# Casts of weights behind exponentials, modulation columns in another bank, and a different scratch tile, in a two-layer transformer block on one core

## The chip, the core and the metric

The kernel runs on one core of a Trainium2 chip. The core has five engines that run side by side, each through its own instruction queue in order: TensorE (PE; matrix products and transposes, results in PSUM), VectorE (DVE), ScalarE (ACT), GpSimd (POOL), and SyncE (SP), which here only issues DMA transfers. Instructions on different engines are ordered by semaphores. The metric is the device time of one execution in microseconds (us), the median of three runs.

## What is computed

The reference is a block of two layers over 512 latent tokens and 256 context tokens with 1024 features, in float32. Cut to what matters here:

```
for l in range(2):
    mx = silu(c) @ mod_w[l] + mod_b[l]          # 6 x 1024 modulation values, for latents
    mc = silu(c_ctx) @ mod_w[l] + mod_b[l]      # the same for the context
    shx1, scx1, gx1, shx2, scx2, gx2 = split(mx, 6)
    hx = rms(x) * norm_mix_w * (1 + scx1) + shx1
    hc = ...                                    # the context, with mc
    layer 0: heads q, k, v = (hx|hc) @ ev_w_in, rms and rotation of q and k,
             half the heads attend in a window of 128 with a sink, half densely;
             joined heads @ ev_w_out
    layer 1: differential attention: (softmax(q0 k0) - lam * softmax(q1 k1)) @ v
    x = x + gx1 * attention
    x = x + gx2 * swiglu(rms(x) * ... , ffn_w_in, ffn_w_out)
    the context likewise, in layer 0 only
return x
```

The modulation gives, per layer, six parts of 1024 values for each of the two streams: shift, scale and gate for the attention (parts 0, 1, 2) and for the feed-forward part (3, 4, 5). They are independent of the tokens, so they are computed piece by piece beside other work.

## The kernel before, in words

**Precision.** A float32 operand is split into a rounded part (hi) and the rest (lo): ACT casts (`nc.scalar.copy(hi, raw)`), then DVE or POOL subtracts (`tensor_sub(lo, raw, hi)`). A product of two such operands is three products on PE: hi*hi, hi*lo, lo*hi. So each weight tile costs one DMA, one cast on ACT and one subtraction, before PE may use it.

**Who sets the order.** Most of the program is ordered by a planner: it simulates the engines and hands out, on each engine, the ready instruction that stands earliest in the program. Its times are its own, so an instruction can be placed ahead of others in a queue and then, on the chip, hold them while it waits. `tc.manual_schedule(engines={PE})` keeps PE in the order of the program text; it is entered at the sixth tile of layer 0's attention (`i == 5`) and holds to the end. `with behind("exp"):` adds, for the instructions of the block that run on ACT, an edge to the last exponential issued so far: in ACT's queue they come after it. Instructions of other engines and DMAs in that block get no edge.

**Layer 0's attention** runs from about 78 to 396 us. It has four blocks b = 0 to 3 of four query heads with one key and value head (b < 2: window, b > 1: dense), and each block goes over six tiles of 128 tokens in the order 4, 5 (context), 0, 1, 2, 3; the last block in the order 0 to 5. The text speaks of blocks 0 to 3 and of a block's first to sixth tile; `j` counts the tiles from 0. In each step:

- `scores0(i)`, four times, one head each: PE writes the scores `sc` to one of two banks (L587, with mask products L589), DVE takes the row maximum (`mx`, `nm`), ACT the exponential (L601, tile `Pt`). After two heads, DVE takes `rc`, the reciprocal of the sums, and POOL scales `Pt` (L613).
- `transposes0(i - 1)`, three times: PE transposes `Pt` of the tile before (`ppt`, L621, in one of two banks tr0 and tr1), and ACT (L626) and DVE (L624) copy it back.
- `values0(i - 1)`: PE multiplies by the values into `av` (L632, bank acc1), ACT copies to `o` (L634).
- `projected(n)`: quarters of the next block's input projection `inps` (L474, bank acc0), each over two of the eight slices of 128 features. A finished tile is copied (`qkv`), rotated by DVE and POOL, split (`qd`, `kd`), and transposed by PE later (`qpt`, `kpt`, also in tr0 and tr1; copied by ACT as `qt`, `kT`).

In the last block there is no next projection; from its fourth tile on, the output projection `ops` of earlier tiles stands there instead, whose result DVE multiplies by a gate row `g` (`rtmp`, L480).

**Input weights.** `weights0` makes the weights of one block in four units of 256 features: cast on ACT (`wihi`, L507), subtraction on POOL (first and third unit) or DVE (second and fourth) (`wilo`, L508). The loads go into raw tiles (tag "raw", two of them). The first two units of block b + 2 are taken at the end of the fifth tile (`j == 4`) of block b, the other two at the start of the next block (`j == 0`); between them, at the end of the sixth tile, a modulation piece uses the same two raw tiles.

**Output weights.** `out_units0` issues eight loads at its first call, then gives one unit per call: cast (`woh`, L801), subtraction on POOL for the first six and on DVE for the last two (`wol`, L802). In block 3 one unit is taken at the end of the first tile, two in the second, three in the third, the rest in the fourth.

**Modulation pieces.** `mod_steps` makes 256 columns in two steps. First: two DMAs (`modw`, L177) into raw tiles, eight row products (x16 in the trace) to a PSUM tile `mod` in the bank given by `bank` (L182), and ACT's copy `modr` (L185). Then: two small products `modcol` (L191, x4 in the trace), in the same bank, and DVE adds the bias (`modc`, L279). `mod_run(n)` does the first step at the end of a tile (`RUNS`), and `mod_ends()` the second, behind the first scores of the next tile. At the end of block 1 and of block 3's first tile `mod_ends()` follows `mod_run` at once.

**The gate.** `gate_mem(0, 2, 2)` transposes gate columns on PE (`gps`, L293), copies them on DVE (`grow`) and writes them to DRAM (`gmem`, SP); `oproj.gates` loads them back to all partitions (`g`, L306), in the first tile of block 3.

**Layer 1's start.** The first head's projection is laid out by hand, with the normalisation of latent tiles 1, 2, 3 between (`last_norm0`). `factors` squares these three tiles first: ACT's squares (L331) write their elements to one tile, `spare`, that nobody reads; only the row sums count. Then for each tile POOL multiplies by the row factor into `h` (L345, shown as `nh`), PE transposes `h` (`npt`, L352), and DVE and ACT apply scale and shift into `hc` (L360, L358). `h` and `hc` are `spare`, tiles of the ring "xo" (six), or a raw tile.

## Time and profile before

| | us |
|---|---|
| median of 3 runs | 1686.9 (1685.64 to 1687.21) |
| the profiled execution | 1686.72 |
| its span (first to last instruction) | 1684.9 |
| PE busy | 1629.0 (97%) |
| DVE busy | 1145.2 (68%) |
| ACT busy | 934.8 (55%) |
| POOL busy | 713.2 (42%) |

The clock that PE was granted is 0.994 on the mean. Rows of a timeline read: start, duration, engine, line of the kernel, operation, output<-inputs, shape, count, and in a bracket the engine's idle time before it with what released it. Rows of waits read: engine, tile and line that waited, whom it waited for, the total in us, how often, and the longest. An ending q (SPq) means the engine's instruction queue. Idle time is put down to the release that came last. PE's products are pipelined, so their durations overlap.

### The profile page before, as it was taken

The page shows a single profiled execution, that of the slowest core. Times are in us where ns is not written, and L with a number is a line of the kernel's source. Part 1 is how long each engine was busy: PE and PEld are TensorE (multiplying, and loading weights), DVE is VectorE, ACT ScalarE, POOL GpSimd, SP SyncE. Part 2 cuts the span into 40 slices and gives each one's busy share as a digit, 9 for nine tenths or more (in the row PEclk, how much of TensorE's full clock was granted, in tenths as well). Part 3 has the DMA queues.
Part 4 walks back from the last instruction along what each step waited for, and adds up shares of the span by engine and source line. Part 5 has one row for each costly group of instructions (what it writes and reads, how often), then busy time and mean ns, then how long its engine had stood idle before and what let it go on. Part 6 is the DMA issues. An engine that isn't in the chain of part 4 may idle for free. (4 is left out here: it accounts for less than half of the span.)

```text
span 1684.9 us, 28521 instructions
## 1 busy us (share of the span) xinstructions
PE 1629.0 (97%) x10376; PEld 1467.9 (87%) x10376; DVE 1145.2 (68%) x1980; ACT 934.8 (55%) x2008; POOL 713.2 (42%) x872
## 2 busy tenths in 40 slices
PE   6999999899999999999999999999999999999998
PEld 3977787677999999998878799999988899999887
DVE  3765756554799987767767666666666598887433
ACT  5466665745455655544564456666666555555320
POOL 2665555621345554412413367766765332221000
PEclk8999999999999999999999999999999999999999
DMA  9221321421455555439965221111113333331431
GB/s 321 70 71 52 93 70 51 163 63 38 120 178 173 166 159 164 135 110 334 305 185 192 91 58 44 48 42 47 45 51 100 113 96 110 104 105 53 138 100 63
DMA packets 221692, 194.67 MB, mean 116 GB/s; under 512 B 20016, under 2 KB 206960, under 8 KB 221552
## 3 DMA queue, kind: packets, MB, share of 16 engines
q1 hardware_dynamic: 221200, 192.65, 36.9%
q8 instruction: 81, 1.33, 0.3%
q14 instruction: 59, 0.48, 0.1%
q10 hardware_dynamic: 352, 0.21, 0.0%
HBM read 179.94 MB, written 12.87 MB: 114 GB/s over the span
## 5 line engine op out<-in xcount | busy, mean ns | idle before, releaser
L928 ACT CAST wbh<-wr 128x512 fp32r<-128x512 f32 x170 | 104.8, 621 | 122.9 <-PE p L960 67.7
L960 PE MATMUL p<-hT,wbh 128*128 128x256 f32 (+1 forms) x752 | 154.1, 298 | 0.0
L474 PE MATMUL inps<-wih,hT 128*128 128x384 f32 x512 | 143.9, 343 | 2.4 <-ACT qkv L688 1.7
L938 POOL TENSOR_TENSOR wbl<-wr,wbh 128x512 fp32r<-128x512 f32 x43 | 58.9, 1369 | 174.2 <-ACT wbh L928 174.2
L960 PEld LDWEIGHTS p<-hT,wbh 128*128 128x128 f32 x752 | 122.1, 191 | 0.2
L938 DVE TENSOR_TENSOR wbl<-wr,wbh 128x512 fp32r<-128x512 f32 x127 | 107.8, 860 | 19.8 <-ACT wbh L928 15.8
L960 PE MATMUL p<-hT,wbl 128*128 128x256 f32 (+1 forms) x376 | 111.8, 297 | 0.0
L960 PE MATMUL p<-t,wbh 128*128 128x384 f32 (+1 forms) x480 | 110.9, 317 | 0.0
L231 POOL TENSOR_TENSOR modp<-modp 128x512 f32<-128x512 f32 x40 | 57.5, 1437 | 111.8 <-ACT modp L230 111.8
L613 POOL TENSOR_SCALAR Pt<-Pt,rc 128x256 f32<-128x256 f32 (+3 forms) x96 | 75.3, 796 | 66.1 <-DVE rc L610 58.5
L960 PE MATMUL p<-hTt,wbh 128*128 128x256 f32 (+1 forms) x480 | 100.9, 302 | 0.0
L914 POOL TENSOR_TENSOR wr<-wr 128x512 f32<-128x512 f32 x40 | 62.2, 1556 | 91.1 <-DVE ws L919 88.8
L474 PEld LDWEIGHTS inps<-wih,hT 128*128 128x128 f32 x512 | 93.4, 188 | 5.4 <-ACT qkv L688 2.8
L960 PE MATMUL p<-b,wbh 128*128 128x384 f32 x368 | 93.5, 335 | 0.6 <-DVE c L988 0.6
L928 ACT CAST wbh<-ws 128x512 fp32r<-128x512 f32 x120 | 69.5, 580 | 43.7 <-PE p L960 28.5
L224 DVE SCALAR_TENSOR_TENSOR ma<-modw,cols,ma 128x256 f32<-128x256 f32 x140 | 91.5, 654 | 2.3
L601 ACT ACTIVATE Pt<-sc,nm 128x256 f32<-128x256 f32 (+3 forms) x96 | 67.7, 708 | 34.0 <-DVE nm L597 16.0
L474 PE MATMUL inps<-wil,hT 128*128 128x384 f32 x256 | 85.8, 335 | 0.0
L938 DVE TENSOR_TENSOR wbl<-ws,wbh 128x512 fp32r<-128x512 f32 x120 | 81.7, 681 | 1.7 <-ACT wbh L928 1.6
L960 PEld LDWEIGHTS p<-t,wbh 128*128 128x128 f32 x480 | 82.8, 189 | 0.0
L960 PEld LDWEIGHTS p<-hTt,wbh 128*128 128x128 f32 x480 | 78.4, 191 | 3.0 <-ACT modp L230 2.1
L474 PE MATMUL inps<-wihi,hT 128*128 128x384 f32 x256 | 76.6, 356 | 2.1 <-DVE modc L279 1.9
(357 smaller groups left out, 5219.1 us busy)
## 6 DMA issues: line engine op xcount, KB each, us to landing
modw<-in_mod_w_dram SPq DMA_DIRECT2D x96, 512.0 KB, 4.8
wr<-in_ffn_w_in_dram SPq DMA_DIRECT2D x176, 256.0 KB, 3.0
wdr<-in_ffn_w_out_dram SPq DMA_DIRECT2D x66, 512.0 KB, 3.6
wir<-in_od_w_in_dram SPq DMA_DIRECT2D x96, 128.0 KB, 2.3
hidm<-hid SPq DMA_DIRECT2D x44, 192.0 KB, 1.9
hr<-hidm SPq DMA_DIRECT2D x22, 192.0 KB, 3.5
x<-in_x_dram SPq DMA_DIRECT2D x8, 512.0 KB, 3.6
wir<-in_ev_w_in_dram SPq DMA_DIRECT2D x16, 256.0 KB, 3.4
```

The lines of the kernel that those rows point to most:

```text
L224: nc.vector.scalar_tensor_tensor(acc, w[:, k], scale[k], acc, ALU.mult, ALU.add)
L231: nc.gpsimd.tensor_add(pr[:, 0:2], pr[:, 0:2], pr[:, 2:4])
L474: nc.tensor.matmul(ps, hs[j][:, k, :], ws[k // 2][z][:, k % 2, c0:c1], start=(k, j, z) == (0, 0, 0), stop=(k, j, z) == (KT - 1, 1, 0))
L601: turn["exp"] = nc.scalar.activation(p[:, :n], s, AF.Exp, bias=nm[:, c1], accum_out=sm[:, c1])
L613: nc.gpsimd.tensor_scalar(p[:, :n], p[:, :n], rc[:, hh:hh + 1], 1.0, ALU.mult, ALU.mult)
L914: nc.gpsimd.tensor_sub(w, raw[f, "G1"], w)
L928: nc.scalar.copy(hi, w)
L938: (nc.gpsimd if name == "G2" else nc.vector).tensor_sub(lo, raw[need[n]], f32(hi))
L960: nc.tensor.matmul(ps, w[:, k, :], H[b][h][:, k, :], start=first and k == 0 and q == 0, stop=final and k == 3 and q == 2, skip_group_check ...
```

## The change

- `mod_steps` takes a bank for the columns (`cols_bank`); `mod_run` gives acc1, so `mod` stays in acc0 and `modcol` is in acc1.
- At the end of block 1 there is no `mod_ends` and no `gate_mem` any more; the columns are made behind the first scores of block 2, the gate's transpose and write at the end of block 3's first tile. The columns of that tile's piece are made behind the first scores of its second tile.
- `weights0`: the third and fourth unit are taken behind the exponentials of the first and second scores of a block's first tile (the first block takes what it has at the start, as before); the first two units in the fifth tile are behind that tile's last exponential.
- `out_units0`: in block 3's second tile the two units move from behind the first and third to behind the second and fourth exponential; in the third tile they stay behind the first three.
- `last_norm0`, tile 1: `h` is a tile of the ring and `hc` is `spare`; it was the other way round.

```diff
-    def mod_steps(l, part, n, new_tile, pool, bank, wide=None, room=("modr", 1)):
+    def mod_steps(l, part, n, new_tile, pool, bank, wide=None, room=("modr", 1), cols_bank=None):
...
-        pc2 = p_1.tile([P, nb, 2], F32, name="modcol", tag=bank)
+        pc2 = p_1.tile([P, nb, 2], F32, name="modcol", tag=cols_bank or bank)
...
-                mod_runs.append(mod_steps(*mods.pop(0), raw_tile, at.pool, "acc0"))
+                mod_runs.append(mod_steps(*mods.pop(0), raw_tile, at.pool, "acc0", cols_bank="acc1"))
...
             if j == 0 and b < 3:
-                ws += units
+                if not b:
+                    ws += units
...
                 scores0(i)
+                if j == 0:
+                    with behind("exp"):
+                        ws += islice(units, 1)
                 mod_ends()
                 transposes0(i - 1)
                 scores0(i)
+                if j == 0:
+                    with behind("exp"):
+                        ws += units
                 projected(n[0])
...
                 if j == 4 and b < 2:
-                    ws = [next(units) for _ in range(2)]
+                    with behind("exp"):
+                        ws = [next(units) for _ in range(2)]
...
                 mod_run(RUNS[b][j])
-                if b == 1 and j == NT - 1:
-                    mod_ends()
-                    gate_mem(0, 2, 2)
...
                 mod_run(1)
-                mod_ends()
                 wp.close()
...
                 ws = [next(units)]
+                gate_mem(0, 2, 2)
                 oproj = OutProj(0, ws, o_t, xs)
...
             scores0(i)
+            mod_ends()
             if t < 3:
+                with behind("exp"):
+                    ws += islice(units, t - 1)
+                transposes0(i - 1)
+                scores0(i)
                 with behind("exp"):
                     ws += islice(units, 1)
                 transposes0(i - 1)
                 scores0(i)
                 with behind("exp"):
                     ws += islice(units, t - 1)
-                transposes0(i - 1)
                 scores0(i)
                 with behind("exp"):
-                    ws += islice(units, 1)
-                scores0(i)
+                    ws += islice(units, 2 - t)
...
     def last_norm0(t):
-        h, hc = (spare if t == 1 and not i else raw_tile([P, KT, P], "nhc") if t == 2 and i else
+        h, hc = (spare if t == 1 and i else raw_tile([P, KT, P], "nhc") if t == 2 and i else
                  keep.tile([P, KT, P], F32, name="nh", tag="xo", bufs=6) for i in range(2))
```

## The prediction, made before the changed kernel ran

> **What bounds the kernel now.** I read the page first, then the busy time by stretches, then what TensorE (PE) waited for between 78 and 396 us, where layer 0's attention runs, and then the timelines of single engines around each wait. "us" is the time from the span's start.
>
> ```profile
> span 1684.9 us, 28521 instructions
> ...
> 80.00:400.00 320.00, 301.86 (x2146) 241.81 (x2144) 190.35 (x436) 190.93 (x469) 164.87 (x234) 1.00 0.25 78
> ...
> 950.00:1290.00 340.00, 328.87 (x2263) 312.30 (x2261) 224.93 (x443) 223.13 (x568) 230.72 (x359) 0.99 0.19 55
> ```
>
> The columns after the stretch's length are PE, weight loads, VectorE (DVE), ScalarE (ACT), GpSimd (POOL), clock, DMA share and GB/s. PE is busy 301.86 of 320 us, at clock 1.00; no other engine passes 60%, and DMA is at 0.25. So PE sets the end, and only its 18.1 idle us can be won in this stage. Which waits make them up:
>
> ```profile
> PE ppt L621 <- ACT qt L546: 4.6, 5, 2.2
> PE ppt L621 <- POOL Pt L613: 2.9, 5, 1.0
> PE sc L587 <- ACT Pt L601: 2.3, 3, 1.3
> PE inps L474 <- DVE modc L279: 1.9, 3, 1.0
> ...
> PE modcol L191 <- ACT modr L185: 1.0, 2, 0.5
> ...
> 96.92 0.44 PE L474 MATMUL inps<-wihi,hT 128*128 128x384 f32 x1 [1.01 <-DVE modc L279]
> ...
> 110.35 0.45 PE L474 MATMUL inps<-wihi,hT 128*128 128x384 f32 x1 [0.65 <-DVE modc L279]
> ...
> 199.18 0.66 PE L621 MATMUL ppt<-cst,Pt 128*128 128x128 f32 x4 [2.20 <-ACT qt L546]
> ...
> 219.97 0.61 PE L191 MATMUL modcol<-cst,modr 128*128 128x2 f32 x4 [0.49 <-ACT modr L185]
> ...
> 225.41 1.10 PE L621 MATMUL ppt<-cst,Pt 128*128 128x128 f32 x8 [0.89 <-ACT qt L546]
> ...
> 303.97 0.96 PE L587 MATMUL sc<-kT,qt 128*128 128x256 f32 x4 [0.49 <-ACT Pt L601]
> ...
> 310.10 0.61 PE L191 MATMUL modcol<-cst,modr 128*128 128x2 f32 x4 [0.55 <-ACT modr L185]
> ...
> 315.97 0.97 PE L587 MATMUL sc<-kT,qt 128*128 128x256 f32 x4 [1.29 <-ACT Pt L601]
> ...
> 322.00 0.33 PE L621 MATMUL ppt<-cst,Pt 128*128 128x128 f32 x1 [0.34 <-POOL Pt L613]
> ...
> 322.88 0.77 PE L621 MATMUL ppt<-cst,Pt 128*128 128x128 f32 x5 [0.55 <-POOL Pt L613]
> ```
>
> In a bracket stands PE's idle time before the row and what released it. From the attention's sixth tile on, PE's order is the program's own, so each such wait moves the rest of the stage unless something else is late behind it. Before that tile the planner orders PE too.
>
> **Part 1, the columns' bank.** The two small products that make the modulation columns, modcol, write acc0 before, so the next projection, also in acc0, waits for DVE to read them: 1.9 us in three waits. After, they write acc1, whose next writer is av at the tile's end, microseconds later; the projection then needs only the copy modr, which modcol itself had to wait for. No instruction is added. I take **-1.9**. Bounds: 0, if another wait stands right behind, and -1.9.
>
> **Part 2, casts of layer 0's input weights.** The first two casts of the set loaded during block 1 are planned into its fifth tile, in front of an exponential:
>
> ```profile
> 194.90 0.83 ACT L507 CAST wihi<-wir 128x768 fp32r<-128x768 f32 x1 [0.63 <-DMA wir<-in_ev_w_in_dram]
> ...
> 197.03 0.83 ACT L507 CAST wihi<-wir 128x768 fp32r<-128x768 f32 x1 [0.79 <-issue]
> 197.77 0.79 ACT L601 ACTIVATE Pt<-sc,nm 128x640 f32<-128x640 f32 x1
> ...
> 198.55 0.57 ACT L546 CAST qt<-qpt 128x512 fp32r<-128x512 f32 x1
> ...
> 195.81 1.82 POOL L508 TENSOR_TENSOR wilo<-wir,wihi 128x768 fp32r<-128x768 f32 x1 [1.76 <-ACT wihi L507]
> ...
> 196.07 1.84 DVE L535 TENSOR_TENSOR qd<-qy,qd 128x256 fp32r<-128x256 f32 x1 [1.01 <-ACT qd L534]
> ...
> 210.14 0.43 DVE L535 TENSOR_TENSOR qd<-qy,qd 128x256 fp32r<-128x256 f32 x1 [0.27 <-ACT qd L534]
> ...
> 203.52 0.81 ACT L601 ACTIVATE Pt<-sc,nm 128x640 f32<-128x640 f32 x1
> ...
> 218.41 1.07 PE L182 MATMUL mod<-modw,s_pad 128*32 128x256 f32 x16
> ...
> modw<-in_mod_w_dram SPq DMA_DIRECT2D x4, 512.0 KB, 3.5
> ```
>
> ACT stands 0.63 us for the load and 0.79 us before the second cast; with 2 x 0.83 us of casts that is 3.08 us in front of exp and qt, and the copy qt (end 199.12) holds the bank that the transposes at 199.18 want. With the edge both casts come after this tile's last exponential, the one at 203.52, some 7 us later. Without them qt would be through about 2 us or more sooner, and PE reaches the transposes at 196.98. I take **-2.0** of the 2.20. What the late casts hold: their weights aren't read before the next block, but the raw tiles they free are wanted by the next modulation load (modw on SP's queue, 3.5 us to land, products at 218.4); casts from 204.3 on and a subtraction of 1.82 leave until 218.41 some 12 us, of which the load takes 3.5, so the sixth tile's work covers it. If that cover were gone PE would wait in the mod products.
>
> In block 0 the same two casts were planned into the fourth tile:
>
> ```profile
> 110.61 0.84 ACT L507 CAST wihi<-wir 128x768 fp32r<-128x768 f32 x1 [1.69 <-DMA wir<-in_ev_w_in_dram]
> ```
>
> ACT loses 1.69 us there, but PE has projections to do meanwhile; I take **-0.3**, bounds 0 and -1.7.
>
> The third and fourth cast, in a block's first tile, already follow exponentials in the trace, and they hang on a load that can't start before the modulation products have released its raw tile:
>
> ```profile
> 223.58 0.83 ACT L507 CAST wihi<-wir 128x768 fp32r<-128x768 f32 x1 [0.93 <-DMA wir<-in_ev_w_in_dram]
> 224.49 1.82 POOL L508 TENSOR_TENSOR wilo<-wir,wihi 128x768 fp32r<-128x768 f32 x1 [2.20 <-ACT wihi L507]
> ...
> 226.99 0.35 PE L474 MATMUL inps<-wilo,hTc 128*128 128x384 f32 x1
> ```
>
> **Part 3, the columns a tile later.** At the end of block 1 the change takes modcol and the gate's transpose out of the spot at 219.97, where PE idled 0.49 us for modr; behind the next tile's scores modr is long done. Then 0.89 us at 225.41, which sits behind the cast at 223.58, could go too. But here something is late next: the products end at 219.48, the load ends 4.1 us after them, cast and POOL subtraction end at 226.31, and PE reads wilo at 226.99. Whatever PE gains in this tile, it can't read before 226.31: of the 1.38 us at most **0.68** is left, and nothing if cast and qt keep their order. I take **-0.3** for both waits.
>
> At the start of block 3 the same move saves the 0.55 us at 310.10. There the changed casts of the output weights help as well:
>
> ```profile
> 313.50 1.04 ACT L801 CAST woh<-wor 128x1024 fp32r<-128x1024 f32 x1
> ...
> 318.71 2.36 POOL L802 TENSOR_TENSOR wol<-wor,woh 128x1024 fp32r<-128x1024 f32 x1
> ...
> 310.04 3.00 SPq L306 DMA_DIRECT2D g<-gmem  x2
> ...
> 339.71 0.69 DVE L480 TENSOR_TENSOR rtmp<-ops,g 128x512 f32<-128x512 f32 x1 [0.81 <-PE ops L836]
> ```
>
> In the second tile the cast at 313.50 stands ahead of the second exponential, and scores wait 1.29 us for that. The tile before, without such a cast, waits 0.49 at 303.97; so 0.80 goes. Later the subtraction at 318.71 keeps POOL from scaling Pt, 0.34 + 0.55 us at 322; with the casts behind the second and fourth exponential the scaling comes first, or so I read it. Together 0.55 + 0.80 + 0.89 = 2.24; modcol (two products) now lies inside the tile and the gate's transpose is issued here, so I take **-1.9**, bounds -0.5 and -2.2. The gate's round trip through DRAM is now behind the eight weight loads on SP's queue: a write of 8 KB, and the two g loads, issued at 310.04 before, wait for it to land. Behind them stand only the x loads. First use is the rtmp at 339.71, nearly 30 us later, so projections and scores cover it; nothing is charged. If g were later than that, PE would stall at the second output sum.
>
> **Part 4, layer 1.**
>
> ```profile
> 948.88 0.55 POOL L160 TENSOR_TENSOR rs_n<-rs_n,neghalf 128x1 f32<-128x1 f32 x1
> ...
> 953.21 1.06 ACT L331 ACTIVATE nh<-x 128x1024 f32<-128x1024 f32 x1 [1.91 <-DVE x L481]
> ...
> 954.47 1.12 POOL L345 TENSOR_SCALAR nh<-x,rs_n 128x1024 f32<-128x1024 f32 x1 [2.25 <-ACT nh L331]
> ...
> 955.64 1.09 PE L352 MATMUL npt<-cst,nh 128*128 128x128 f32 x8 [1.34 <-POOL nh L345]
> ```
>
> The squares of tiles 1 to 3 all write `spare` as waste, and the scaled rows of tile 1 are written there too; so POOL's scaling at 954.47 waits for tile 3's square (953.21 + 1.06), though tile 1's own factor was done at 949.43. After, the scaled rows have a tile of their own and `spare` takes what is written after the transposes. The scaling can then run before 952, and PE's 1.34 us goes. What comes next is the following weight product, whose operands are there. **-1.3**, bounds 0 (if the other tile of the ring weren't free) and -1.34.
>
> **A price for what is new.** A moved cast is still 0.83 us (1.04 for the output weights) of ACT and 1.82 or 2.36 of POOL somewhere else. No row shows it at its new place. Bounds: nothing, if it fills idle time (ACT is free 40% of the stage), and 2.20 a place, as in block 1's fifth tile. Five places change: block 0's and block 1's fifth tile, the first tiles of blocks 1 and 2, block 3's second. I take **+1.5**, two waits a little under the 0.89 of 225.41: that row is the nearest, a cast behind an exponential, as all are after the change.
>
> Here a rule speaks against the change. The row: DVE's subtraction qd took 1.84 us beside POOL's wilo and ended with it, against 0.43 alone. The Trainium skill, page "SBUF — State Buffer", section "Who interferes with whom", says that a DVE instruction with two SBUF inputs and a GpSimd instruction that reads SBUF exclude each other for a whole instruction; the trace agrees with 1.84 against 0.43. By it each of the five moved subtractions could cost DVE 1.4 us; if PE paid all of that, 7.0 would stand in place of the 1.5 and the sum would be -0.7.
>
> **Sum.** -1.9 - 2.0 - 0.3 - 0.3 - 1.9 - 1.3 + 1.5 = -6.2 us. The profiled execution took 1686.72 us (1684.9 of span and 1.8 around it), the median of the runs is 1686.9: 1680.5 on the one, **1680.7** on the other. Gains hold to the end, since PE runs at 97% in 950 to 1290 us and only a load late by microseconds could eat them.
>
> **Rivals.**
> - **Floors and the planner eat the layer-0 gains.** ACT, DVE and POOL are ordered by the planner anew; the edge only forbids a cast ahead of an exponential, which in the first tiles already holds, so there the change does nothing. If the waits at 199 and 316 turn into others of the same size, the bank (1.9) and layer 1 (1.3) stay, less 1.5: -1.7, **1685.2**. For it: the floor at 226.31, and POOL's part in the waits. Against: the 2.20 us has two plain culprits that leave. Chance 0.27.
> - **Slower: moved casts and subtractions stall PE where they land.** Place: the end of each fifth tile and the sixth tile behind it, and the like in blocks 2 and 3. A 1.82 us subtraction on POOL holds DVE's two-input additions of the projection as qd was held (1.4 us), the row maximum queued behind them on DVE comes late, the exponential and the score bank after it, and PE waits as at 199.18. Price 2.20 in five places is 11.0, against gains of 7.7: +3.3, **1690.2**. It decides from 1.54 us a place. Against: a tile's third scores stand behind eight transposes and half a projection, which gives the first exponential slack. Chance 0.11.
> - **More goes than the named waits.** Of the 4.6, 2.9 and 2.3 us in the list of waits the rows name 3.09, 0.89 and 1.78; 4.0 us are other waits for the same qt, Pt and exp. If 3 of them go with the rest, and no new wait comes, it is 10.7: **1676.2**. Chance 0.10.
>
> **How the numbers follow.** Forecast (-9 to -3.4 us) 0.52. About 0.2%, 3.4 us, is what a measurement of this kernel can tell from no change. Faster by more: 0.52 + 0.10 = 0.62; within it 0.27; slower 0.11. The range leaves out half of the larger gain and most of the slower case: 1676.5 to 1688.5.
>
> **What would show it.** In the changed profile: no wait of modcol's bank or modr before inps and modcol (part 1, 3); no wait above 0.5 us for qt in block 1's fifth tile, and its two casts behind the fourth exponential (part 2); inps still reading wilo about 7 us after the mod products (the floor); the wait for the exponential near 314 at 0.5 us; the transposes of layer 1's tile 1 without a wait for nh (part 4). Wrong if PE waits for weight casts in the sixth tiles, for modw, or for g, or if PE's planned order before the sixth tile comes out longer.

## The result, and the profile after

The changed kernel is slower: 1687.62 us (median of 21 runs, 1683.95 to 1693.22), the kernel before beside it 1684.61 us (21 runs, 1681.51 to 1688.07), ratio **1.002**, interval 1.0012 to 1.0027. A second series of the same two kernels gave 1687.97 and 1685.33 us, 1.0009 (1.0000 to 1.0018). Forecast was -6.2 us; measured are +1.5 to +3.4.

The page's first line of the changed kernel, and the stretches that were shown of before (same columns: length, busy us and count of PE, weight loads, DVE, ACT, POOL, then clock, DMA share, GB/s):

```profile
span 1685.0 us, 28524 instructions
```

```profile
80.00:400.00 320.00, 301.32 (x2122) 239.07 (x2121) 190.21 (x427) 188.69 (x465) 161.62 (x230) 0.99 0.24 76
950.00:1290.00 340.00, 328.89 (x2268) 312.97 (x2266) 225.14 (x444) 223.00 (x568) 230.55 (x360) 0.99 0.19 56
```

The two profiled spans agree to 0.1 us, though the medians differ by 3 us. The reason lies ahead of the first changed place: the change has nothing to do in the first 78 us, but in the changed kernel's profiled execution the clock was better there. The first 78 us of before, then of the changed kernel:

```profile
0.00:78.00 78.00, 62.09 (x394) 50.03 (x394) 41.57 (x83) 39.94 (x80) 29.03 (x46) 0.89 0.67 212
```

```profile
0.00:78.00 78.00, 61.48 (x410) 49.08 (x411) 44.27 (x91) 42.17 (x86) 31.75 (x50) 0.93 0.67 212
```

At 0.93 instead of 0.89 it came to the attention's first scores 2.89 us sooner (75.81 against 78.70). That is no gain of the change: in the profile of x3 below, whose code up to layer 1 is that of before, the first scores start at 75.77. So I count both from there, as in all comparisons of profiles below. Starts of PE's rows in the two traces; the last column is the difference less -2.89:

```
                                     before    after    counted from first scores
first scores of layer 0               78.70    75.81     0
mod products, end of block 0         144.65   142.31    +0.55
mod products, block 1's fourth tile  190.00   187.41    +0.30
mod products, end of block 1         218.41   218.17    +2.65
mod products, block 3's first tile   308.48   308.29    +2.70
first output products                333.15   334.03    +3.78
layer 1's first projection           951.18   952.17    +3.88
layer 1's first scores               992.97   991.32    +1.24
its 129th scores                    1150.49  1150.59    +2.99
end                                 1684.93  1684.99    +2.95
```

The loss has three places: block 1's fifth and sixth tile (+2.35), block 3 (+1.08), the first half of layer 1's attention (+1.75). Only layer 1's start gains (-2.64).

How far can such a count be trusted? There is a second profile of each code. That of the changed kernel (a2 below) has the same +2.35 and +1.08 in the same two places of layer 0, but +0.62 for +1.75 in layer 1's attention. For before it is x3: up to layer 1 all four engines do the same instructions in the same order, and still x3 stands at +0.42 at the end of block 0, at +0.63 at the first output products and at +2.77 at layer 1's first projection. So the two losses in layer 0 are the code's, while +0.55 at the end of block 0 is not told from chance.

What PE waited for in layer 0's attention, 78 to 396 us:

```profile
PE ppt L621 <- POOL Pt L613: 4.1, 5, 1.4
PE ppt L621 <- DVE Pt L624: 3.3, 3, 1.7
PE av L632 <- DVE Pt L624: 2.2, 3, 1.6
PE sc L587 <- ACT Pt L601: 2.0, 5, 0.5
PE ppt L621 <- ACT qt L546: 1.6, 4, 0.6
```

The named waits did go: qt fell from 4.6 to 1.6 us, and no row has modc or modr. In their place stand late Pt tiles: POOL's scaling 2.9 to 4.1 us, DVE's copies from 0.3 to 3.3 us (ppt) and from 1.2 to 2.2 (av). The first place in the timeline, by engine:

```profile
198.37 0.81 ACT L601 ACTIVATE Pt<-sc,nm 128x640 f32<-128x640 f32 x1
...
199.15 1.57 ACT L507 CAST wihi<-wir 128x768 fp32r<-128x768 f32 x2
200.61 0.22 ACT L607 ACTIVATE es<-es 128x2 f32<-128x2 f32 x1
...
200.06 1.81 POOL L508 TENSOR_TENSOR wilo<-wir,wihi 128x768 fp32r<-128x768 f32 x1 [2.41 <-ACT wihi L507]
...
203.92 1.80 POOL L613 TENSOR_SCALAR Pt<-Pt,rc 128x640 f32<-128x640 f32 x2 [1.13 <-DVE rc L610]
...
200.75 1.94 DVE L508 TENSOR_TENSOR wilo<-wir,wihi 128x768 fp32r<-128x768 f32 x1 [3.38 <-ACT wihi L507]
202.62 0.19 DVE L608 TENSOR_TENSOR sm<-sm,es 128x2 f32<-128x2 f32 x1
...
203.67 0.15 DVE L610 RECIPROCAL rc<-sm 128x2 f32<-128x2 f32 x1
...
204.78 0.33 PE L621 MATMUL ppt<-cst,Pt 128*128 128x128 f32 x1 [1.43 <-POOL Pt L613]
205.78 0.77 PE L621 MATMUL ppt<-cst,Pt 128*128 128x128 f32 x5 [0.67 <-POOL Pt L613]
```

Both casts run right behind the last exponential, as the edge says. But the tile isn't done with that exponential: the small one of the sink, es, stands behind it, and now behind 1.57 us of casts. DVE needs es for the sum, the sum for rc, POOL needs rc to scale Pt, PE needs Pt. And before DVE comes to the sum it does its own wilo, 1.94 us beside POOL's; between the sum (202.62) and rc (203.67) stands another 0.9 us of the projection's rotation. So the scaling starts at 203.92, some 5 us after the exponential. Behind it (length, PE, weight loads, DVE, ACT, POOL, clock):

```profile
200.00:205.00 5.00, 2.91 (x22) 1.52 (x18) 4.25 (x10) 2.42 (x6) 3.80 (x4) 1.00 0.20 61
205.00:210.00 5.00, 4.33 (x22) 4.04 (x22) 2.79 (x7) 2.54 (x7) 3.69 (x6) 0.66 0.43 149
```

PE is busy 2.91 of 5 us, and then its clock is 0.66 for 5 us: in the trace's clock record a stretch at half from 206.4, 3.41 us long, so about 1.7 us more where PE sets the pace.

### The profile page after: what moved, and what is told of

It is laid out like the page before. It is cut to its first block, busy times and chain, and to the rows that moved or that the text cites. A ratio compares the mean times of both kernels' runs of the same rounds, so it can differ in the third digit from the quotient of the medians.

```text
span 1685.0 us, 28524 instructions
## 1 busy us (share of the span) xinstructions
PE 1628.6 (97%) x10376; PEld 1465.5 (87%) x10376; DVE 1144.8 (68%) x1980; ACT 935.2 (56%) x2008; POOL 712.5 (42%) x872
## 5 line engine op out<-in xcount | busy, mean ns | idle before, releaser
L938 DVE TENSOR_TENSOR wbl<-wr,wbh 128x512 fp32r<-128x512 f32 x127 | 107.8, 858 | 19.6 <-ACT wbh L928 15.9
L230 ACT ACTIVATE modp<-modw,cols 128x256 f32<-128x256 f32 x160 | 68.4, 499 | 16.2 <-POOL ma L236 8.7
```

What stands on the lines that cost most here:

```text
L230: nc.scalar.activation(pr[:, k], w[:, k], AF.Copy, scale=scale[k])
L938: (nc.gpsimd if name == "G2" else nc.vector).tensor_sub(lo, raw[need[n]], f32(hi))
```

## The experiments

Theory one: the moved casts and the columns hold up small operations on ACT and DVE whose results PE needs. Rivals: the loss is spread and by chance; it lies in one block alone; it lies in the half clock or in loads whatever the waits are. All times, with the kernel before in the same series:

| run | us, median (runs) | before | ratio, interval |
|---|---|---|---|
| x1, casts not behind | 1689.22 (12) | 1685.85 | 1.0021, 1.0008 to 1.0035 |
| x2, block 3 as before | 1688.58 (9) | 1685.85 | 1.0014, 1.0001 to 1.0027 |
| x3, squares alone | 1684.55 (12) | 1685.85 | 0.9994, 0.9983 to 1.0004 |
| x4, casts behind alone | 1694.11 (6) | 1685.85 | 1.0058, 1.0044 to 1.0071 |
| y1, casts behind es | 1686.75 (12) | 1685.33 | 1.0008, 0.9996 to 1.0020 |
| a2, changed again | 1687.97 (12) | 1685.33 | 1.0009, 1.0000 to 1.0018 |
| x5, without casts and block 3 | 1687.89 (12) | 1685.33 | 1.0008, 0.9994 to 1.0022 |
| x6, bank alone | 1690.34 (12) | 1685.33 | 1.0022, 1.0009 to 1.0035 |
| z1, y1 with block 3 as before | 1683.83 (11) | 1685.57 | 0.9987, 0.9979 to 0.9996 |
| z2, es and squares | 1683.30 (11) | 1685.57 | 0.9987, 0.9978 to 0.9996 |
| z3, code shifted | 1694.81 (5) | 1685.57 | 1.0053, 1.0039 to 1.0066 |
| z5, z2 with first tiles' casts | 1683.44 (11) | 1685.57 | 0.9985, 0.9976 to 0.9994 |
| x7, columns back | 1685.66 (1) | 1684.89 | |
| x8, casts back | 1689.49 (1) | 1684.89 | |
| w1, without bank | 1690.38 (5) | 1684.89 | 1.0034, 1.0020 to 1.0049 |
| w2, best without bank | 1682.28 (12) | 1685.92 | **0.9979**, 0.9969 to 0.9988 |
| w3, changed kernel mended | 1683.16 (12) | 1685.92 | **0.9981**, 0.9971 to 0.9991 |

**x4, the fifth tiles' casts alone**, on the kernel before:

```diff
                 if j == 4 and b < 2:
-                    ws = [next(units) for _ in range(2)]
+                    with behind("exp"):
+                        ws = [next(units) for _ in range(2)]
```

> The kernel before with one part alone: the first two units of the fifth tiles of blocks 0 and 1 are cast behind the last exponential. The wait of 2.20 us for qt at 199.18 should go in every theory. Theory one (collisions): it is repaid with GpSimd's and VectorE's operations running against each other in the same tile, late Pt copies, and a half clock of 3.41 us behind them: +1.5 to +2.4 us beside the kernel before. Theory two (spread, chance): -1.0 to +0.7 us. The prediction's step gave -2.3 us for it before any price of new stalls.

Far worse than any theory said. Its timeline in block 0's fifth tile:

```profile
131.41 1.55 ACT L507 CAST wihi<-wir 128x768 fp32r<-128x768 f32 x2
132.87 0.20 ACT L607 ACTIVATE es<-es 128x2 f32<-128x2 f32 x1
...
132.99 1.93 DVE L508 TENSOR_TENSOR wilo<-wir,wihi 128x768 fp32r<-128x768 f32 x1 [1.61 <-ACT wihi L507]
134.85 0.15 DVE L608 TENSOR_TENSOR sm<-sm,es 128x2 f32<-128x2 f32 x1
...
132.31 1.80 POOL L508 TENSOR_TENSOR wilo<-wir,wihi 128x768 fp32r<-128x768 f32 x1 [1.44 <-ACT wihi L507]
...
135.29 1.57 POOL L613 TENSOR_SCALAR Pt<-Pt,rc 128x640 f32<-128x640 f32 x2 [1.19 <-DVE rc L610]
...
136.15 0.47 PE L621 MATMUL ppt<-cst,Pt 128*128 128x128 f32 x1 [4.48 <-POOL Pt L613]
```

The same order as in block 1, and here it reaches PE in full: 4.48 us, and a half clock of 3.41 us at 136.2. Counted from the first scores it is 4.81 us late at the end of block 0 and 7.88 at the end of block 1.

**x1, those casts as before**, all else as in the change (the diff of x4 backwards):

> The changed kernel, with one part undone: in the fifth tiles of blocks 0 and 1 the first two units are cast as before, not behind the last exponential. Theory one (the moved casts collide): in the changed kernel's trace ScalarE does both casts in a row (1.57 us for the two), then GpSimd's 1.81 us subtraction and VectorE's wilo run against each other, and TensorE waits 1.43 and 0.67 us for GpSimd's Pt copy at 204.78 and 205.78; from there its clock is at half for 3.41 us. From the end of the fifth tile's predecessor to the end of block 1 the changed kernel loses 2.35 us. Without the part this goes: 1.5 to 2.4 us below the changed kernel, so +0.6 to +1.5 us beside the kernel before, and no half clock near 206. Theory two (the loss is spread: any of the new orders costs some tenths, and the half clock near 206 is chance): within 0.7 us of the changed kernel, +2.3 to +3.0 us. Theory three (the loss is in block 3 alone): no difference from the changed kernel, +3.0 us.

Theory one is wrong about the gain: there is none. The profile says why. Without the edge the wait for qt in block 1's fifth tile is back, longer than the 2.20 us of before (2.72 us at 198.53), with the half clock now at 198.0. So the casts cost something in either place: there they hold up qt, behind the exponential they hold up es.

**x2, block 3 as before** (columns at its first tile, old order of the output weights' casts):

> The changed kernel with block 3 as before: the modulation columns at its first tile and the old order of the output weights' casts. Theory one (collisions): in the changed kernel two Pt copies of VectorE come late here (waits of 1.24 us at 313.93 and 1.72 us at 326.14), because a small VectorE operation on two SBUF operands takes 1.89 us beside GpSimd's subtraction, and hT 2.16 us. But the first-tile stall that the change removed (about 0.9 us) comes back. So 0.8 to 1.5 us below the changed kernel: +1.5 to +2.2 us beside the kernel before. Theory two (spread, chance): within 0.7 us of the changed kernel. Theory three (block 3 alone has the loss): 2.5 to 3.0 us below it, at 0 to +0.5 us.

Between the mod products of block 3's first tile and the first output products this profile loses 0.00 us, the changed kernel 1.08. In the place the size fits theory one (0.8 to 1.5 us). The time does not show it: +2.7 us by the medians is theory two's answer, and the interval overlaps the changed kernel's.

**x3, layer 1's squares alone** (the diff's last lines):

> The kernel before with the layer-1 part alone: the other of the two squares of tile 1 goes to the spare tile. Theory one: this part does what was forecast for it, the wait of 1.34 us goes and TensorE reaches layer 1's attention 1.3 to 2.6 us sooner, and this is kept: -1.3 to -2.6 us beside the kernel before. Rival: what layer 1's start gains is lost again at the next loads of weights (in the changed kernel's trace two casts wait 1.94 and 1.75 us for a DMA at 1096 and 1134, and TensorE 0.95 and 1.26 us for them): -0.5 to +0.5 us.

-1.3 us by the medians, and by the interval not told from nothing. In the profile the first scores of layer 1 are 2.4 us sooner against its start, and no weights are late behind it. The rival falls for this part, in this one profile.

**y1, the edge moved by one instruction**, on the changed kernel:

```diff
-                nc.scalar.activation(es_, es_, AF.Exp)
+                turn["exp"] = nc.scalar.activation(es_, es_, AF.Exp)
```

> The changed kernel, with one dependence moved: where a block has the sink, a cast that stood behind the exponential of the scores now stands behind the small exponential of the sink that follows it (es). In the changed kernel's trace the two casts of 1.57 us stand between them, so the sums, their reciprocals and GpSimd's Pt multiplications come 1.5 us later, behind GpSimd's subtraction; and TensorE waits 1.43 and 0.67 us for Pt at 204.78 and 205.78. In the run with this part alone the same order made a wait of 4.48 us at 136.15. Theory one (the casts do harm because they hold up es): these waits go, 1.5 to 3.0 us below the changed kernel, -1.0 to +1.0 us beside the kernel before. Theory two (GpSimd's subtraction of 1.81 us does it, wherever it lies): the wait moves to another Pt and stays within 0.7 us of the changed kernel. Theory three (the changed kernel's loss is in half-clock stretches that come by chance behind any gap of TensorE): no less than 1 us of loss left, and the mean clock of the runs stays at 0.993.

Its timeline at the same place, ACT and POOL, and the stretches:

```profile
199.42 0.21 ACT L607 ACTIVATE es<-es 128x2 f32<-128x2 f32 x1
199.52 1.57 ACT L507 CAST wihi<-wir 128x768 fp32r<-128x768 f32 x2
...
200.20 1.57 POOL L613 TENSOR_SCALAR Pt<-Pt,rc 128x640 f32<-128x640 f32 x2 [2.27 <-DVE rc L610]
201.73 2.53 POOL L508 TENSOR_TENSOR wilo<-wir,wihi 128x768 fp32r<-128x768 f32 x1
```

```profile
200.00:205.00 5.00, 4.34 (x38) 3.12 (x35) 3.91 (x6) 3.28 (x7) 4.45 (x4) 1.00 0.24 70
205.00:210.00 5.00, 3.67 (x28) 3.32 (x26) 3.47 (x11) 2.65 (x9) 2.54 (x5) 1.00 0.45 140
```

The same two casts, the same subtraction; es is first, the scaling starts at 200.20 instead of 203.92, both Pt waits go and so does the half clock (1.00 for 0.66). The end of block 1 is at +0.19 where the changed kernel has +2.65: in this place theory one holds and theory two falls. A smaller wait comes: 1.32 us at 207.24, for a copy of DVE. The time alone does not show it: 1.2 us less than a2's median, where 1.5 to 3.0 were expected, with overlapping intervals. z2 beside x4 shows it below.

**a2, the changed kernel again:**

> The changed kernel once more, without an edit, for a second profile of it. Fixed causes: the same waits as in its first profile to within 0.2 us (Pt at 204.78 and 205.78, 313.93, 326.14; the two late loads of weights near 1096 and 1134, where TensorE waits 0.95 and 1.26 us), a half clock of 3.41 us right behind 206, and +2.5 to +3.5 us beside the kernel before. Chance: the late loads or the half clock lie elsewhere or are gone, and the time lies anywhere from +1.5 to +4 us.

The four Pt waits named come back to within 0.01 us, with a half clock at 207.3: a fixed cause. Of the two late loads only the second came back.

**x6, the bank alone:**

> The kernel before with the columns' bank alone. The prediction's step: the waits of in_proj matmuls for modc (1.7 us in two, up to 1.0) go, -1.9 us. Rival: the columns in the other bank make another order of TensorE's work in block 0, and what was gained there is lost at the next Pt or qt (as in the changed kernel, which is 0.55 us later at the end of block 0 in spite of it): -0.5 to +0.7 us.

Worse than the rival: +5.0 us by the medians. The profiled execution is the slowest of its twelve (1694.24 us). PE's rows:

```profile
105.75 0.86 PE L587 MATMUL sc<-kT,qt 128*128 128x256 f32 x4 [1.31 <-ACT Pt L601]
...
108.02 0.69 PE L474 MATMUL inps<-wihi,hT 128*128 128x384 f32 x1 [1.28 <-ACT modr L185]
...
200.37 1.12 PE L621 MATMUL ppt<-cst,Pt 128*128 128x128 f32 x4 [3.10 <-ACT qt L546]
```

In place of 1.01 and 0.65 us for modc stand 1.31 and 1.28, the second for the copy modr, which ACT does behind a cast that waits 1.07 us for its load; 2.20 became 3.10. Half clock follows at 107.5 (3.41 us) and 199.7 (6.83 us). At the end of block 1 it is 6.20 us late, of which by estimate 5.1 are the 10.24 us at half clock. PE's order before the sixth tile, which is the planner's, comes out otherwise: where modcol and then 18 products of the projection stood (from 95.41 in before), 24 products stand now, and modcol comes later.

**x5, bank, first tiles' casts, later columns of block 1, and squares** (the casts of x4 and block 3 undone):

> The changed kernel with two parts undone: the casts of the fifth tiles and all of block 3. What is left: the columns in another bank, the casts of block 1's and 2's first tiles behind the exponentials, block 1's last columns a tile later, and layer 1's squares. If the loss is in the two parts undone (each of them alone gave little: +3.4 and +2.7 us by medians where the changed kernel had +3.0), this is -1.5 to 0 us beside the kernel before, layer 1's part alone being worth -1.3. If the loss is in what is left, or in the half clock that comes with it, +1.5 to +3.5 us.

By the medians the second answer (+2.6 us), by the interval not told from nothing. The profile is clearer: +3.71 us at the end of block 1, with 1.68 us at 107.10 and 3.01 at 200.04, as in x6. Up to block 3 x5 has the instructions of x1 in the same order, and x1 is at +1.65 there: 2 us between two executions of one code, one with a half clock at 107.8, the other without.

**w1, the changed kernel without the bank:**

> The changed kernel with the columns in the old bank. If holding up es is what costs, and the order that the new bank gives was what kept it small in block 0: the stall of over 4 us in block 0's fifth tile, as with these casts alone, is back, and the run is 3 to 7 us above the kernel before. If the bank is a loss wherever it is: 1 to 3 us below the changed kernel, with layer 1's two loads landing in under 3 us.

The stall of x4 is back: 4.48 us at 132.60. So the bank's worth hangs on where the casts stand: with casts behind the exponential its order takes most of that stall in block 0 away, with the casts as before it makes new ones.

**x7 and x8, block 3 in two halves**, on the changed kernel. x7 puts the columns back, x8 the casts:

```diff
x7:                 mod_run(1)
+                mod_ends()
                 wp.close()
...
             scores0(i)
-            mod_ends()
             if t < 3:
```

> The changed kernel with block 3's modulation columns at its first tile again, the output weights' casts in the new order. If the small aff operation of VectorE (1.89 us beside GpSimd's wol, 0.16 before) makes the first late Pt copy and the moved wol the second: the wait of 1.24 us at 314 goes, the first-tile wait of about 1.3 us for kT at 316 comes back, and the wait of 1.72 us at 326 stays. If the aff operation makes both, both go.

> The changed kernel with the output weights' casts in the old order, block 3's columns in the second tile. If the order of the casts makes the wait of 1.72 us at 326: it goes, and 0.4 to 0.6 us waits as in the kernel before stand there. The wait of 1.24 us near 314 stays if the aff operation meets the subtraction in the old order too; if it goes, it needs both steps.

First the changed kernel's timeline, then x7's, then x8's (POOL, DVE, PE):

```profile
310.88 2.37 POOL L802 TENSOR_TENSOR wol<-wor,woh 128x1024 fp32r<-128x1024 f32 x1 [2.04 <-ACT woh L801]
...
322.02 2.37 POOL L802 TENSOR_TENSOR wol<-wor,woh 128x1024 fp32r<-128x1024 f32 x1
...
311.38 1.89 DVE L283 SCALAR_TENSOR_TENSOR aff<-modc,cols 128x4 f32<-128x4 f32 x1
313.19 0.68 DVE L624 COPY Pt<-ppt 128x512 f32<-128x512 f32 x1
...
323.32 2.16 DVE L820 TENSOR_TENSOR hT<-o,hT 128x1024 fp32r<-128x1024 f32 x1
325.40 0.68 DVE L624 COPY Pt<-ppt 128x512 f32<-128x512 f32 x1
...
313.93 0.66 PE L621 MATMUL ppt<-cst,Pt 128*128 128x128 f32 x4 [1.24 <-DVE Pt L624]
...
326.14 0.66 PE L621 MATMUL ppt<-cst,Pt 128*128 128x128 f32 x4 [1.72 <-DVE Pt L624]
```

```profile
312.59 0.14 DVE L283 SCALAR_TENSOR_TENSOR aff<-modc,cols 128x4 f32<-128x4 f32 x1
...
316.70 0.96 PE L587 MATMUL sc<-kT,qt 128*128 128x256 f32 x4 [0.50 <-ACT Pt L601]
...
325.67 1.09 PE L621 MATMUL ppt<-cst,Pt 128*128 128x128 f32 x8 [0.79 <-ACT Pt L626]
```

```profile
313.55 1.90 DVE L283 SCALAR_TENSOR_TENSOR aff<-modc,cols 128x4 f32<-128x4 f32 x1
...
316.11 0.66 PE L621 MATMUL ppt<-cst,Pt 128*128 128x128 f32 x4 [1.25 <-DVE Pt L624]
```

aff works on 128x4 numbers and takes 0.16 us by itself (before, at 301.03); begun half a microsecond into POOL's wol it ends with it, after 1.89 us, and the copy behind it is late. The columns make this first wait, in either order of casts. The second needs both halves: DVE's hT beside the wol at 322.02 took 2.16 us (1.34 in x7); with either half undone a wait of 0.8 us for a copy of ACT stands in its place. From block 3's first tile to the output products x8 loses 0.07 us, both halves 1.08, and x7, the new casts without the columns, **gains** 0.99. x7's expectation was wrong in one point, and it matters: the wait for the second exponential didn't come back in full (1.29 before, 0.50). The times of x7 and x8 are of one run each and tell nothing apart; the waits do: those of 1.24 and 1.7 us stand in all six profiles that have both halves.

**z3, 124 tiny products (248 products and 248 weight loads in the trace) at the start of TensorE's code**, where it waits for its first rows:

```diff
     pcol = tr_tile("pcol", [P, 48])
+    for _ in range(124):
+        nc.tensor.matmul(pcol[0:32, 0:2], ident[:, 0:32], ident[:, 0:2], start=True, stop=True)
     nc.tensor.transpose(pcol, rows, ident[0:48, 0:48])
```

> The changed kernel with 124 tiny matmuls (32x2, overwritten by the transposes behind them) ahead of TensorE's first transposes, where it waits for the rows. Nothing else changes but the place of TensorE's code. In all seven profiles with the columns' bank two loads of weights in layer 1 land 3.4 to 4.5 us after their issue instead of 2.3, and in each of them a packet of code of 16 KB starts while they are under way (1094.33 and 1131.29 in the changed kernel); in the three profiles without it the packet starts 2.1 to 2.3 us behind the issue, and they land in 2.1 to 2.7. TensorE's stream has 10515 instructions there and 10512 here. 248 more make 251, which is 5 short of a packet's 256. Theory one (the code's packet delays the loads): the two packets come some 1 to 2 us later beside the loads, the loads land in under 3 us, and the waits of 0.95 and 1.26 us at 1098.69 and 1136.85 go: 1.5 us gained between layer 1's first and last scores. Rival (the loads are late for another reason, and the packets are by chance there): the waits stay. The whole time may be up to 3 us longer from the matmuls themselves at the start, or differ by the half clock there.

It is about layer 1's late weights. PE's rows and the answer on the tile wir in 1040 to 1160 us, of the changed kernel; then that answer of z3:

```profile
1098.69 0.39 PE L474 MATMUL inps<-wih,hTc 128*128 128x256 f32 x1 [0.95 <-ACT qkv L688]
...
1136.85 0.39 PE L474 MATMUL inps<-wil,hTc 128*128 128x256 f32 x1 [1.26 <-POOL wil L380]
```

```profile
  DMA wir<-in_od_w_in_dram: 4.8, 4
...
DMA to landing us min/median/max: 2.1/2.3/4.5
```

```profile
  DMA wir<-in_od_w_in_dram: 2.6, 5
...
DMA to landing us min/median/max: 2.1/2.3/2.9
```

ACT's casts wait 4.8 us for these loads in the changed kernel, 2.6 in z3, where no load takes over 2.9 us and none of PE's waits there over 0.4 us: between the first and the 129th scores z3 gains 0.28 us against before, the changed kernel loses 1.75. The packets of code (16 KB) beside the loads, from the trace's DMA records:

```
kernel    load issued   packet starts behind it   load lands behind it
before      1096.70            2.15                     2.16
before      1130.55            2.19                     2.26
changed     1092.54            1.79                     4.02
changed     1129.82            1.47                     3.77
w3          1129.28            1.26                     3.57
z3          1139.57            2.10                     2.42
```

So the theory holds for this place, in one profile; from layer 1's first projection on, over 200 us, all four engines do the changed kernel's instructions in its order. Ahead of that they don't, and there the expectation is wrong: the planner, with 124 products more, orders the start and block 0 of the attention otherwise. The whole run was 9 us longer, far over the 3 us allowed for: in the profile 3.46 of them arise within 15 us of the attention's start (a new wait of 1.35 us at 85.20 and half clock at 86.1) and 3.2 more by the end of block 0. The expectation's count of instructions is one of weight loads without the products. With both, z3 adds 495 rows, and the trace has 83 packets of code of 16 KB instead of 81.

All eleven other profiles with the bank have one or both loads late; of those without it only w1 has one (3.96 us). So the bank is one way to shift the code, not the only one. One thing the theory does not explain: the latest loads of all, 4.5 to 4.6 us in the changed kernel (1091.83), x8 and z1, have their packet only 2.4 to 2.5 us behind the issue, when other loads had landed.

**z1, z2, z5, combinations on the theory:**

> The changed kernel with the casts behind es and with block 3 as before. If the parts add up: the casts behind es took the two Pt waits away (2.35 us by the end of block 1 in the profile), block 3 as before takes 0.75 us more (from block 3's start to the first output product 0.02 us is lost instead of 1.08). So 3.1 us less than the changed kernel's profile by the first output product, counted from the start of the attention: +0.6 us beside before there; over the runs -0.5 to +1.0 us beside the kernel before, since the late loads of layer 1 (1.75 us) stay. If half-clock stretches decide whatever the waits are: +1.5 to +3 us.

> The kernel before with layer 1's part and the casts of the fifth tiles, but behind es; the columns' bank, the first tiles' casts, the columns a tile later and block 3 as before. Theory one (holding up es was what made these casts cost +8.3 us alone): the waits of 4.48 us at 136 and 1.42 us at 211 go, and with them the 2.20 us wait for qt; -1.3 (squares) -1.0 to -2.5 (casts): -2 to -4 us beside the kernel before. Theory two (the casts' subtraction on GpSimd is what costs): -1.0 to +3 us. Layer 1's loads are not late here, if that comes with the columns' bank.

> The kernel of the casts behind es and layer 1's squares, with the first tiles' casts behind exponentials as well (blocks 1 and 2). If these casts only smooth the start of a block: within 0.5 us of the kernel without them, -2 to -4 us beside before. If they too meet GpSimd's multiplications: 0.7 to 2 us above it, with Pt waits at 152 to 160 or 222 to 230 us that the other doesn't have.

All three are faster than the kernel before. z1 is the changed kernel with two things mended: the first output products are at +0.34 (expected +0.6) and the time -1.7 us by the medians (expected -0.5 to +1.0); its two loads in layer 1 are late still (PE waits 1.25 and 0.94 us). z2 shows that the casts of x4, behind es, cost nothing that can be seen: 4.48 us became 1.36 and 0.45, and the run, which has the squares' gain too (-1.3 alone, x3), is at -2.3 us instead of +8.3, with intervals far apart. z5 is the same as z2.

**w2 and w3, what the places predict together.** w2 is z5 with the new order of the output weights' casts; w3 is the whole change with casts behind es and block 3's columns back:

> The kernel before with layer 1's squares, the first tiles' casts behind exponentials, the fifth tiles' behind es, and the new order of the output weights' casts; no other bank and no later columns. If the places add up: like z5 (-2.2 us by means), and 1.0 us more from the order of the output weights' casts with block 3's columns at the first tile (x7): -2.5 to -4 us beside the kernel before. If half-clock stretches and packets of code undo it: -1 to -2.5 us.

> The changed kernel with casts behind es and block 3's columns at its first tile; bank, later columns of block 1, and the new order of the output weights' casts as in the change. If the places add up: z1 (-2.4 us by means) and 1.0 us more from the order of the casts: -2.5 to -4 us beside the kernel before, the two late loads of layer 1 (1.5 us) still in it. If the cause is elsewhere: -1 to +1 us.

Both faster by 0.2%, by the medians -3.6 us (w2) and -2.8 us (w3). The changed kernel and w3 differ in one `turn["exp"] =` and one moved `mod_ends()`. y1 and w3 differ in that `mod_ends()` alone: 1.0008 (0.9996 to 1.0020) and 0.9981 (0.9971 to 0.9991) beside the kernel before.

## Why the prediction was wrong

- **Part 1, the bank (-1.9).** The waits for modc went, as said. The step that failed is "I take -1.9" with no bound above 0: it took PE's order in block 0 as given, though the text knew that the planner orders PE there and named a longer order as a sign of being wrong. In x6 waits of 1.31 and 1.28 us stand in place of 1.01 and 0.65, and the run is +5.0 us by the medians, much of it half clock behind longer waits. In the whole change block 0 ends at +0.55, no gain, though not told from chance.
- **Part 2, casts (-2.0, -0.3).** The wait of 2.20 us for qt went, and the weights' users had cover, as said: neither wilo nor modw was ever waited for. What failed is the sentence that the casts come after "this tile's last exponential" and the check of what they hold there: it looked at raw tiles and the next block and not at es, the next row on ACT. That exponential's tile had its sum, reciprocal and scaling still to come. x4 and y1 show it.
- **Part 3, columns a tile later (-0.3, -1.9).** Block 1 to 2: the 0.49 us went, as forecast, 0.77 us gained by the next mod products (end of block 2's second tile), and 0.81 lost again in the third and fourth, where PE waits 0.69 us for kT at 265.57. Block 3: the casts gained 0.99 us (x7) of the 1.69 in the sum. The 0.80 at the second exponential came (1.29 to 0.50); of the 0.89 for the scaling 0.34 went and 0.55 stayed. What failed is that the columns inside the tile were charged as "two products": they bring a DVE operation on two SBUF operands, which met POOL's wol (1.89 for 0.16 us). With it block 3 is +1.08 where -1.9 was taken. The gate's later round trip cost nothing, as said.
- **Part 4, squares (-1.3).** Right in its cause, and low: layer 1's start gained 2.64 us, in x3 2.4. The wait of 1.34 us is gone, one of 0.62 fell to 0.28 (only to 0.58 in x3); where the rest came from wasn't followed. In the time x3 has -1.3 us, not told from nothing. The scaling is through at 951.64 instead of 955.59, 3.5 us ahead of the transposes, which have no bracket now (POOL, PE):

```profile
950.52 1.12 POOL L345 TENSOR_SCALAR nh<-x,rs_n 128x1024 f32<-128x1024 f32 x1
...
955.12 1.04 PE L352 MATMUL npt<-cst,nh 128*128 128x128 f32 x8
```

  "Gains hold to the end ... only a load late by microseconds could eat them": two loads came late and ate 1.75.
- **The price of new stalls (+1.5)** was the term off by most: x4's part without the bank is +8.3 us, and in the change the fifth and sixth tile of block 1 lose 2.35 us where 2.0 were to be won. The second rival had the right kind and place of it, the end of the fifth tile, the bound of 2.20 us, which x4 passed with 4.48, was too low, and its route was another: not qd on DVE and the next maximum, but es on ACT, wilo on DVE and the scaling on POOL of the same tile. That its sum, +3.3 us, lies near the measured +3.0 is luck: it set five stalls of 2.20 us against gains of which most did not come. In the rows DVE operations beside POOL's were long, as the rival has it: 1.94 us for wilo (0.95 in block 0), 1.89 for aff (0.16), 2.16 for hT (1.34). The Trainium skill, page "SBUF — State Buffer", section "Who interferes with whom", states the rule for it: a DVE instruction with two inputs in SBUF and a POOL instruction that reads SBUF exclude each other. These rows agree with it. The rival's chance of 0.11 was too small: the prediction applied the rule to the five moved subtractions, beside the sum, but not to aff, which the moved columns bring, nor to the two halves of one split, which now ran against each other.
- **Not in the sum at all:** half clock behind a stall, by estimate 1.7 us for each 3.41 us, and packets of code beside loads.

Summed by place, from the profiles: +0.30 to block 1's fourth tile, +2.35 in its fifth and sixth, +0.05 in block 2, +1.08 in block 3, +0.10 up to layer 1, -2.64 at its start, +1.75 in its attention, -0.04 after: +2.95. That this is also the difference of the medians (3.0) is partly chance, since one execution of each kernel stands behind it; a2's profile gives +2.68.

## What to carry to other kernels

An edge "behind the exponential" must name the last small instruction of the chain that feeds TensorE, not the last big one: ask what stands next in that queue, and who needs it. Before a tiny two-operand VectorE instruction is moved, look what GpSimd does at its new place. Time each edit alone: here the squares did what was forecast and the output weights' order more than half of it, the input weights' casts and block 3's columns did harm only by where their instructions landed, and the mended change is faster than both kernels.

## What the hardware showed that was not expected

- **Half clock at a bunch of idle time.** PE's granted clock is recorded as 1 or 0.5, the latter in the attention in stretches of 3.41 us or twice that. In all eight profiles with two waits for Pt of some 1.43 and 0.5 to 0.7 us within a microsecond, a stretch began within 2 us of them. It did so too at the single waits of 2.72, 3.01, 3.10 and 4.48 us (twice), but not at the 2.20 of before and the 2.34 of x3; and in w2 one began at 133.2, behind 1.36 us at 131.68, where z2 and z5 with the same wait had none, and in w1 one some 2 us behind the 1.71 at 330.02, where five other profiles with that wait had none. So a longer stall mostly costs 1.7 us (an estimate, half of 3.41) more than its own length, and a shorter one sometimes. It makes the runs scatter as well: of the changed kernel's 21 runs the two at mean clock 0.988 took 1691.5 and 1693.2 us, the four at 0.995 or above 1684.0 to 1686.8.
- **Loads beside a packet of code land late.** Between 1088 and 1145 us of all profiles, each load of layer 1's weights with a 16 KB packet of code starting 0.5 to 1.3 us behind its issue landed in 3.3 to 4.1 us instead of 2.3; with 1.4 to 1.9 us some did (4.02 in the changed kernel), some not (2.33 in z2 at 1.60). No load without such a packet within 2.5 us landed late. TensorE has 20891 rows of instructions in every kernel with the bank but z3, 20888 or 20889 in the others, some 258 to each of the 81 packets: two or three instructions more in layer 0 went with late weights 800 us later. z3 supports for this place that the code's position decides; why so few are enough stays open.
